# A norm's row factors fetched through DRAM, and the first unit's scaling moved behind its results

## The chip, the core and the metric

The kernel runs on one core of a Trainium2 chip. The time is device microseconds of one execution of the whole program, lower is better. Its matrix products are done by TensorE, elementwise work by VectorE, ScalarE and GpSimd; transfers are issued from the queues of SyncE (called SP), ScalarE and GpSimd (called POOL).

## What is computed

One layer of a hybrid encoder for 1024 rows of width 1024, all in float32. Three token mixers run on a normed input, are gated, summed and projected, and are added to the input; then comes a second norm and a convolutional gated mixer. The change lies where the second part begins:

```python
merged = (gates[:, :, 0] * (y_a @ w_br_hgrn) + gates[:, :, 1] * (y_b @ w_br_fox)
          + gates[:, :, 2] * (y_c @ w_br_mem))
x = x + merged @ w_out
h2 = x * rsqrt(mean(x * x, axis=-1) + EPS) * norm_ffn_g        # the second norm
a, v = split(h2 @ w_up, 2)                                     # the way up, 1024 -> 2 x 2816
a = causal_depthwise_conv3(a) + conv_b
x = x + (gelu(a) * v) @ w_down                                 # the way down
```

## The kernel before

Activations lie transposed: 128 channels on the partitions, the 1024 rows of the sequence along the free dimension, so a factor for each row of the sequence is a vector along the free dimension that every partition needs a copy of. That is `r2`, a tile of 128 x 1024 in which all partitions hold the same 1024 numbers. The norm is applied after the products: the way up multiplies the unnormed `x1` (times the norm's gain), and its results are multiplied by `r2`.

Each float32 operand is split into a rounded high part (a cast, mostly on ScalarE, line 166, or L166 through `operand_parts`) and a low part (a subtraction, mostly on VectorE, L174 or L1350), and one product is three matmuls (`mm3`, L160 to L162): high by high, and the two mixed ones. The weights' parts are the tiles `wh` and `wl`.

The way up goes in units. A unit makes two output blocks of 128 channels for all 1024 rows, by seven block products instead of eight (a scheme of Strassen's kind): the operands on the activations' side are seven families (`B11`, `T1`, `T2`, `B22`, `T3`, `B21`, `T4`), those on the weights' side `o1` to `o7`, sums of four blocks `a11`, `a12`, `a21`, `a22` that are loaded as the tile `rw`. One product is four blocks of `mm3`, 12 matmuls. There are 11 pairs of units; the first unit of a pair makes the convolution's rows (`at`, tiles `fa`), and the second the values (`put_v`). Results leave the PSUM banks through `put_a(c, n, ps, e)`, where `c` is the output block, `n` the half of the rows, `ps` the bank and `e` a copy of an earlier state of that bank. A bank goes on being added to after it was read: the product T4 adds to the bank that `put_a(1, 1, ...)` reads.

In the first unit things are drawn together. The products B11, T1 and T2 run while the last block of `x1` is still being finished; between T1 and T2, `second_norm` sums the squares (L1416, 8 products with a column of ones into 128 x 8) and `rstd_small` makes `rt2`, the factors as 8 columns of 128 (L178 on VectorE, L179 on GpSimd). `families` then makes the parts of the four other families. After the third, T3, `spread` makes `r2` from `rt2`: eight products of a column, broadcast along the free dimension, with the identity (L366), and two copies out of PSUM by ScalarE (L368). The rows `fa` lie where the first operands lay, so `new_rows` and all of `put_a` come after the families.

The order of instructions on each engine is written when the kernel is built, by a planner with a model of the times; program order is its priority. It is held in places by `tc.issue_after(ins)`, which keeps what follows behind `ins` on the engine of `ins`. In `families` T4 is kept behind the last operand of the first unit (`late["o7"]`), and the first operand of the second unit is kept behind the last low part of T4 (`late["last"]`). `acc`, the sum of squares, shares its tile with `r2`. The first norm's factors take a road through DRAM in `spread_dma` (L353 to L359): transposed to a row of 8 x 128, written, and read back to all partitions.

Of the kernel before, what the change touches and what calls it, by code (L numbers as in the profile page):

```python
# [8 lines left out]
F32 = mybir.dt.float32  # L9
F32R = mybir.dt.float32r  # L10
AF = mybir.ActivationFunctionType
ALU = mybir.AluOpType
AX = mybir.AxisListType

P = 128
T = 1024
D = 1024
KC = D // P
HB = 512
# [90 lines left out]
def tile_block(ctx: ExitStack, tc: tile.TileContext, xT, memT, x_rows, mem_rows, vec, fbias, mats, hmask, w_first, w_cm, w_hi, w_fqk, w_fv,  # L110
               w_mkv, w_br, w_out, w_up, w_dn, w_pair, outT):
    nc = tc.nc
    V, S, G, PE, SP = nc.vector, nc.scalar, nc.gpsimd, nc.tensor, nc.sync
# [17 lines left out]
    def ps_tr():  # L131
        return pz.tile([P, HB], F32, tag="tr", name="tr", bufs=2)

    def ps_po():
        return pz.tile([P, HB], F32, tag="po", name="po", bufs=1)
# [3 lines left out]
    ident = cp.tile([P, P], F32, tag="ident", name="ident")  # L139
# [36 lines left out]
    def rstd_small(out, ss, n):  # L176
        w = ss.shape[1]
        late["mean"] = V.tensor_scalar(out, ss, 1.0 / n, EPS, ALU.mult, ALU.add)  # L178
        return G.tensor_tensor(out, out, mhalf[:, :w], ALU.pow)  # L179
# [173 lines left out]
    def spread_dma(r, rcol, row, name, ps):  # L353
# [3 lines left out]
        rd = tc.dram_tile([1, T], F32, name=f"{name}_d")  # L357
        SP.dma_start(rd.rearrange("o (a b) -> (o a) b", a=8), row)
        SP.dma_start(r, rd.partition_broadcast(P))  # L359

    def spread(r, rcol):

        for n in range(2):
            ps = ps_tr()
            for b in range(4):
                PE.matmul(ps[:, b * P:(b + 1) * P], rcol[:, 4 * n + b:4 * n + b + 1].to_broadcast([P, P]), ident,  # L366
                          start=True, stop=True)
            S.copy(r[:, n * HB:(n + 1) * HB], ps)  # L368


    pkv = {}

# [131 lines left out]
    def family_block(name, k, src, sub=None):  # L504
        h, l = fam[name]
        return split(S, h[k], l[k], src, sub)
# [52 lines left out]
    class Dense:  # L559
# [11 lines left out]
        def sum_of(self, i, a, b, t=None):  # L571
            t = t if t is not None else home["sums"].tile([P, HB], F32, tag=f"s{i}", name=f"s{i}")
            V.tensor_add(t, a, b)
            return t

        def operand(self, src):
            if self.half is None:
                self.half = [wp.tile([P, 4 * 264], F32R, tag=t, name=t, bufs=3) for t in ("wh", "wl")]
                h, l = (t[:, :HB] for t in self.half)
            else:  # L580
                h, l = (t[:, HB:2 * HB] for t in self.half)
                self.half = None
            split(S, h, l, src)
            return h, l
# [746 lines left out]
    r2 = pr.tile([P, T], F32, tag="r2", name="r2")  # L1331
# [40 lines left out]
    for i, j in enumerate((0, 4, 1, 5, 2, 6, 3, 7)):  # L1372
# [6 lines left out]
        for n, ps in chunk:  # L1379
            sl = slice(n * HB, (n + 1) * HB)  # L1380
            dst = sum7 if i == 7 else x1[j]
# [29 lines left out]
    rt2 = cp.tile([P, 8], F32, tag="rt2", name="rt2")  # L1411

    def second_norm():
        ps = ps_po()
        for tb in range(8):
            PE.matmul(ps[:, tb:tb + 1], acc[:, tb * P:(tb + 1) * P], ones[:, 0:1], start=True, stop=True)  # L1416
        rstd_small(rt2, ps[:, :8], D)


    def snap(ps):  # L1420
# [4 lines left out]
    def first_products(o1, o2, o3, between=None):  # L1425
        x, y = ps_proj(), ps_lg()
        product(x, o1, "B11", True)
        e1 = snap(x)
        product(y, o2, "T1", True)
        e5 = snap(y)  # L1430
        late["e5"] = late["snap"]
        if between:
            between()
        product(x, o3, "T2", False)
        return x, y, e1, e5, snap(x)
# [16 lines left out]
    def unit(src, put, begun=None, before=None, after=None, ahead=None):  # L1452


        raw = pw.tile([P, 4, HB], F32, tag="rw", name="rw", bufs=2)
        for i in range(2):
            late["raw"] = G.dma_start(raw[:, 2 * i:2 * i + 2, :], src[:, 2 * i:2 * i + 2, :])  # L1457
        a11, a21, a22, a12 = (raw[:, i, :] for i in range(4))
        if begun:
            x, y, e1, e5, e2, o4 = begun  # L1460
            o5 = operand(sum_of(3, a11, a21))
            late["o5"] = late["cast"]
            o6, o7 = operand(a12), operand(a22)
            late["o7"] = late["cast"]
            before()
        else:
            with tc.issue_after(after.ins) if after else nullcontext():
                o1 = operand(a11)
                with tc.issue_after(late["split"].ins):
                    s1 = sum_of(1, a21, a22)  # L1470
                o2 = operand(s1)
            s2 = sum_of(2, s1, a11)
            x, y, e1, e5, e2 = first_products(o1, o2, operand(s2))
            o4 = operand(sum_of(4, s2, a12))
            o5 = operand(sum_of(3, a11, a21))
        product(y, o4, "B22", False)
        put(0, 1, y, e2)
        if not begun:
            o6 = operand(a12)
        product(x, o5, "T3", False)  # L1480
        put(1, 1, x, e5)
        if not begun:
            o7 = operand(a22)
        if ahead:
            ahead()
        z = ps_tr()
        product(z, o6, "B21", True)
        put(0, 0, z, e1)
        product(x, o7, "T4", False)
        put(1, 0, x, None)  # L1490
# [4 lines left out]
    def families():  # L1495

        for name, q, after in (("B22", 3, None), ("T3", 1, "e5"), ("B21", 2, "snap"), ("T4", 0, "snap")):
            with ExitStack() as order:
                if after:
                    order.enter_context(tc.issue_after(late[after].ins))  # L1500
                if after == "snap":
                    order.enter_context(tc.issue_after(late["split"].ins))
                    order.enter_context(tc.issue_after(late["o7" if name == "T4" else "o5"].ins))
                for k in range(4):
                    late["last"] = family_block(name, k, quarters(k)[q], G if name == "B21" and k > 1 else None)
            if name == "T3":
                spread(r2, rt2)
        px.release()
        late["pq"] = Rounded(tc, name="pq", bufs=1, side="right", reuse_waits="tile")

# [33 lines left out]
    for p in range(NF // 2):  # L1544
        at = []

        def new_rows():
            for _ in range(2):
                t = late["pq"].tile([P, T + 2], F32, tag="fa", name="fa", bufs=3)
                V.memset(t[:, 0:2], 0.0)  # L1550
                at.append(t)

        def rest():
            families()
            new_rows()

        def put_a(c, n, ps, e):
            sl = slice(n * HB, (n + 1) * HB)
            dst = at[c][:, 2 + n * HB:2 + (n + 1) * HB]
            src = ps  # L1560
            if e is not None:
                V.tensor_add(dst, ps, e)
                src = dst
            if c:
                V.scalar_tensor_tensor(out=dst, in0=src, scalar=-1.0, in1=r2[:, sl], op0=ALU.mult, op1=ALU.mult)
            else:
                V.tensor_mul(dst, src, r2[:, sl])

        if p:
            new_rows()  # L1570
            unit(w_up[2 * p], put_a)
            next(sums, None)
        else:
            unit(w_up[0], put_a, begun, rest)
        pq = late["pq"]
        cs = []
        for i in range(2):
            f = 2 * p + i
            c = pq.tile([P, T], F32, tag="fc", name="fc", bufs=4)
            w = [col(C_CW + t * NF + f) for t in range(3)]  # L1580
            S.activation(c, at[i][:, 2:], AF.Identity, bias=col(C_CB + f), scale=w[2])
            V.scalar_tensor_tensor(out=c, in0=at[i][:, 1:T + 1], scalar=w[1], in1=c, op0=ALU.mult, op1=ALU.add)
            V.scalar_tensor_tensor(out=c, in0=at[i][:, 0:T], scalar=w[0], in1=c, op0=ALU.mult, op1=ALU.add)
            S.activation(c, c, AF.Gelu)
            V.tensor_mul(c, c, r2)
            cs.append(c)

        def put_v(c, n, ps, e):
            dst = cs[c][:, n * HB:(n + 1) * HB]
            src = ps  # L1590
            if e is not None:
                V.tensor_add(e, ps, e)
                src = e
            if c:
                V.scalar_tensor_tensor(out=dst, in0=src, scalar=-1.0, in1=dst, op0=ALU.mult, op1=ALU.mult)
            else:
                V.tensor_mul(dst, src, dst)
            SP.dma_start(yd[:, 2 * c + n, p, :], dst)

        unit(w_up[2 * p + 1], put_v, after=None if p else late["last"],  # L1600
             ahead=down_operands if p == NF // 2 - 1 else None)
        for _ in range(1 + (1 <= p < 4)):
            next(sums, None)
        t1 = pq.tile([P, HB], F32, tag="ft", name="ft")
        V.tensor_sub(t1, cs[0][:, :HB], cs[0][:, HB:])
        SP.dma_start(yd[:, 4, p, :], t1)
# [62 lines left out]
    for a, b, own, first, c, n, sign, last, xq in (  # L1669
# [6 lines left out]
        dst = banks if own else ybanks  # L1676
# [138 lines left out]
```

## Time and profile before

| What | Value |
|---|---|
| Time, median of 3 runs | 1698.82 us (1698.47 to 1700.21) |
| The profiled execution's own time | 1700.23 us |
| Its span, first to last instruction | 1698.4 us |
| Granted TensorE clock over the span | 0.999 |
| TensorE busy | 1691.0 us |
| VectorE busy | 1150.8 us |
| ScalarE busy | 800.9 us |
| GpSimd busy | 324.6 us |

In the rows of the profile below, PE is TensorE, DVE is VectorE, ACT is ScalarE; "L366" is line 366 of the program. A row of a timeline gives start and length in us, engine, line, operation, output <- inputs and their shapes, and in brackets how long the engine idled before it and for whom. Tile names lose their numbers: `rt` stands for `rt2` too, `r` for `r2`, `x` for `x1`.

### The profile page before, as it was taken

The numbers are of one execution on the slowest core, as the hardware profiler recorded it, in microseconds if no ns is written. First come the engines' busy times: TensorE is split into PE (matmuls) and PEld (weight loads), VectorE is DVE, ScalarE is ACT, GpSimd is POOL, SyncE is SP. The second block draws the span as 40 slices with busy tenths as digits, with TensorE's granted clock in tenths as the row PEclk, the third lists the DMA queues.
The fourth block names the chain that finished last, engine by engine and source line by source line (L and its number), as shares of the span: only waits on it lengthen the run. The fifth ranks groups of instructions, "written<-read, shape, count | busy, mean of one in ns | idle before, by whom it ended". The sixth has DMA issues, their size and how long they took to land.

```text
span 1698.4 us, 24291 instructions
## 1 busy us (share of the span) xinstructions
PE 1691.0 (100%) x8957; PEld 1452.4 (86%) x8957; DVE 1150.8 (68%) x2057; ACT 800.9 (47%) x1428; POOL 324.6 (19%) x420
## 2 busy tenths in 40 slices
PE   9999999999999999999999999999999999999999
PEld 7888899989898998888888888888888888888887
DVE  6966455666666664886856845987878888775654
ACT  6734455545454553775631333644434444533432
POOL 0200032543433331544310000311111111100000
PEclk9999999999999999999999999999999999999999
DMA  9443232221212111110346542566544344494772
GB/s 367 157 161 106 88 139 68 77 92 51 94 59 77 63 46 57 67 32 13 106 127 209 167 186 100 165 174 169 158 139 138 118 149 143 172 363 145 251 269 87
DMA packets 83062, 227.16 MB, mean 134 GB/s; under 512 B 9712, under 2 KB 12408, under 8 KB 82816
## 3 DMA queue, kind: packets, MB, share of 16 engines
q1 hardware_dynamic: 64320, 160.54, 26.8%
q0 software_dynamic: 18048, 64.50, 13.2%
q8 instruction: 70, 1.15, 0.3%
q10 hardware_dynamic: 576, 0.59, 0.1%
q14 instruction: 48, 0.39, 0.1%
HBM read 180.72 MB, written 67.93 MB: 146 GB/s over the span
## 4 chain that ended last, share of the span: by engine, by line
PE 99%; DVE 0%; ACT 0%; DMA 0%; issue 0%; ACTq 0%; DVEq 0%
PE pp L160 21%; PE pp L162 21%; PE pp L161 21%; PE lg L160 4%; PE lg L162 4%; PE lg L161 4%; PE tr L162 3%; PE tr L161 3%; PE tr L160 3%; PE po L966 1%; PE lg L925 1%; PE lg L924 1%; PE po L965 1%; PE po L160 1%; PE po L161 1%; PE po L162 1%
## 5 line engine op out<-in xcount | busy, mean ns | idle before, releaser
L160 PE MATMUL pp<-uh,wh 128*128 128x512 f32 x412 | 163.3, 396 | 0.0
L161 PE MATMUL pp<-ul,wh 128*128 128x512 f32 x412 | 162.9, 395 | 0.0
L162 PE MATMUL pp<-uh,wl 128*128 128x512 f32 x412 | 162.5, 394 | 0.0
L161 PE MATMUL pp<-wl,uh 128*128 128x256 f32 (+1 forms) x512 | 146.3, 286 | 0.0
L162 PE MATMUL pp<-wh,ul 128*128 128x256 f32 (+1 forms) x512 | 146.1, 286 | 0.0
L160 PE MATMUL pp<-wh,uh 128*128 128x256 f32 (+1 forms) x512 | 145.6, 286 | 0.0
L166 ACT CAST wh<-s 128x512 fp32r<-128x512 f32 x110 | 66.5, 621 | 131.6 <-PE pp L161 55.1
L166 ACT CAST wh<-raw 128x1024 fp32r<-128x1024 f32 (+2 forms) x76 | 67.6, 890 | 100.6 <-PE pp L161 86.2
L166 ACT CAST wh<-rw 128x512 fp32r<-128x512 f32 x87 | 53.2, 619 | 108.1 <-PE pp L161 70.2
L160 PEld LDWEIGHTS pp<-wh,uh 128*128 128x128 f32 x512 | 97.3, 190 | 1.2
L161 PEld LDWEIGHTS pp<-wl,uh 128*128 128x128 f32 x512 | 97.4, 190 | 1.0
L162 PEld LDWEIGHTS pp<-wh,ul 128*128 128x128 f32 x512 | 97.4, 190 | 0.9
L1457 POOL DMA_DIRECT2D rw<-in_w_up x44 | 24.1, 555 | 372.4 <-DVE wl L1350 171.3
L166 ACT CAST dwh<-wr 128x1024 fp32r<-128x1024 f32 (+1 forms) x41 | 40.2, 980 | 115.8 <-PE tr L161 40.0
L162 PEld LDWEIGHTS pp<-uh,wl 128*128 128x128 f32 x412 | 77.5, 188 | 15.1
L174 DVE TENSOR_TENSOR wl<-raw,wh 128x1024 fp32r<-128x1024 f32 (+2 forms) x75 | 78.0, 1040 | 17.8 <-ACT wh L166 17.6
L160 PEld LDWEIGHTS pp<-uh,wh 128*128 128x128 f32 x412 | 77.5, 188 | 14.6
L161 PEld LDWEIGHTS pp<-ul,wh 128*128 128x128 f32 x412 | 77.5, 188 | 14.5
L940 ACT ACTIVATE pt<-pt,st 128x128 f32<-128x128 f32 (+3 forms) x64 | 49.7, 777 | 41.7 <-DVE st L937 33.9
L174 DVE TENSOR_TENSOR dwl<-wr,dwh 128x1024 fp32r<-128x1024 f32 (+1 forms) x41 | 46.3, 1129 | 31.7 <-ACT dwh L166 31.7
L942 POOL TENSOR_SCALAR pt<-pt,st 128x128 f32<-128x128 f32 (+3 forms) x64 | 49.1, 767 | 78.4 <-DVE st L941 64.1
L1350 DVE TENSOR_TENSOR wl<-rw,wh 128x512 fp32r<-128x512 f32 x69 | 47.7, 704 | 22.7 <-PE pp L162 18.2
(500 smaller groups left out, 5123.2 us busy)
## 6 DMA issues: line engine op xcount, KB each, us to landing
rw<-in_w_up POOLq DMA_DIRECT2D x44, 512.0 KB, 4.7
sd<-in_w_dn POOLq DMA_DIRECT2D x30, 512.0 KB, 6.0
br<-yd SPq DMA_DIRECT2D x30, 512.0 KB, 5.0
raw<-in_w_cm SPq DMA_DIRECT2D x24, 512.0 KB, 3.4
gd<-gt SPq DMA_DIRECT2D x48, 256.0 KB, 2.0
gt<-gd SPq DMA_DIRECT2D x48, 256.0 KB, 2.7
yd<-fc SPq DMA_DIRECT2D x44, 256.0 KB, 2.2
wr<-sd SPq DMA_DIRECT2D x20, 512.0 KB, 4.5
```

Source lines behind the costliest of these rows:

```text
L160: PE.matmul(ps, lh, rh, start=first, stop=False, skip_group_check=more)
L161: PE.matmul(ps, lh, rl, start=False, stop=False, skip_group_check=more)
L162: return PE.matmul(ps, ll, rh, start=False, stop=last, skip_group_check=more)
L166: return S.copy(out, in_)
L174: return (sub or V).tensor_sub(l, src, h.bitcast(F32))
L924: PE.matmul(ps[:, :w], qa[i][:, tsl], kh[i][:, s0:s0 + w], start=True, stop=False)
L925: fox_sets[p][3] = PE.matmul(ps[:, :w], qa[i][:, tsl], kl[i][:, s0:s0 + w], start=False, stop=True)
L940: S.activation(pt[:, :ns], pt[:, :ns], AF.Exp, bias=st[:, 2:3], accum_out=st[:, 3:4])
L942: G.tensor_scalar(pt[:, :ns], pt[:, :ns], st[:, 3:4], 0.0, ALU.mult, ALU.add)
L965: PE.matmul(o, vhl[:, sb, :], ph[:, src], start=(sb == 0), stop=False)
L1350: late["split"] = V.tensor_sub(l, src, h.bitcast(F32))
L1457: late["raw"] = G.dma_start(raw[:, 2 * i:2 * i + 2, :], src[:, 2 * i:2 * i + 2, :])
```

## The change

Three edits. `spread`, its eight products and its two copies go. `second_norm` instead writes `rt2` to a DRAM row of 1024 numbers, column by column, and reads that row back to all partitions as `r2`; both transfers are issued from SP. And in the first unit, `put_a` no longer multiplies by `r2`: it copies or adds into the row, and after the unit the two rows are multiplied whole, one of them with the sign turned. The other units are as before.

```diff
-    def spread(r, rcol):
-
-        for n in range(2):
-            ps = ps_tr()
-            for b in range(4):
-                PE.matmul(ps[:, b * P:(b + 1) * P], rcol[:, 4 * n + b:4 * n + b + 1].to_broadcast([P, P]), ident,
-                          start=True, stop=True)
-            S.copy(r[:, n * HB:(n + 1) * HB], ps)
...
         rstd_small(rt2, ps[:, :8], D)
+        rd = tc.dram_tile([1, T], F32, name="r2_d")
+        SP.dma_start(rd.rearrange("o (b p) -> (o p) b", p=P), rt2)
+        SP.dma_start(r2, rd.partition_broadcast(P))
...
-            if name == "T3":
-                spread(r2, rt2)
...
         def put_a(c, n, ps, e):
             sl = slice(n * HB, (n + 1) * HB)
             dst = at[c][:, 2 + n * HB:2 + (n + 1) * HB]
+            if p == 0:
+                if e is None:
+                    S.copy(dst, ps)
+                else:
+                    V.tensor_add(dst, ps, e)
+                return
...
             unit(w_up[0], put_a, begun, rest)
+            V.tensor_mul(at[0][:, 2:], at[0][:, 2:], r2)
+            V.scalar_tensor_tensor(out=at[1][:, 2:], in0=at[1][:, 2:], scalar=-1.0, in1=r2, op0=ALU.mult, op1=ALU.mult)
```

## The prediction

> **What bounds the kernel.** I read the page first: the busy rows and the chain of waits.
>
> ```profile
> span 1698.4 us, 24291 instructions
> ...
> PE 1691.0 (100%) x8957; PEld 1452.4 (86%) x8957; DVE 1150.8 (68%) x2057; ACT 800.9 (47%) x1428; POOL 324.6 (19%) x420
> ...
> PE 99%; DVE 0%; ACT 0%; DMA 0%; issue 0%; ACTq 0%; DVEq 0%
> ```
>
> TensorE is busy for all but 1698.4 - 1691.0 = 7.4 us, and the chain that ends last lies on it for 99% of the span. So whatever the change does to VectorE, ScalarE or the queues counts only if TensorE waits for it, and whatever it takes off TensorE counts in full, unless TensorE then waits for something else at that place. The second view is the list of stages.
>
> ```profile
> 1074.80:1089.00 14.20, 14.02 (x70) 11.45 (x69) 13.01 (x24) 7.68 (x16) 6.46 (x8) 1.00 0.68 194
> 1089.00:1113.00 24.00, 24.00 (x107) 19.88 (x106) 22.63 (x34) 13.75 (x21) 4.88 (x8) 1.00 0.76 198
> 1113.00:1200.00 87.00, 87.00 (x385) 72.06 (x384) 68.64 (x103) 35.46 (x54) 14.04 (x23) 1.00 0.61 168
> ```
>
> The columns are the stage's length, then the busy time of TensorE, weight load, VectorE, ScalarE and GpSimd, the granted clock, the DMA share and GB/s. The change works in the first two rows. There TensorE has one hole (14.20 - 14.02) and VectorE is nearly as full as TensorE: 13.01 of 14.20 us, then 22.63 of 24.00. So VectorE is the engine that could come to set the pace. Which wait ended last in that stage is told by the chain in order of time (start, length, owner), the third view.
>
> ```profile
> 1072.29 0.59 ACT fe L1422
> 1072.88 0.60 ACT wh L166
> 1073.47 2.09 ACT B21h L166 x4
> 1075.56 0.53 ACT wh L166
> 1076.15 0.51 issue
> 1076.89 1.77 DVE wl L1350
> 1079.19 0.68 DVE B21l L174
> 1079.87 2.41 DVE T4l L174 x4
> 1082.28 0.61 DVE wl L1350
> ```
>
> From 1072.29 to 1082.28 + 0.61 = 1082.89 the chain is not on TensorE at all. It leaves TensorE when the third product's result is out, goes through ScalarE's casts of the families and VectorE's low parts, and comes back with the low part `wl` of the second unit's first weights. The eight products of `spread` lie inside this stretch:
>
> ```profile
> 1077.30 0.39 PE L162 MATMUL pp<-T3h,wl 128*128 128x512 f32 x1
> 1077.53 1.95 PE L366 MATMUL tr<-ident,rt 128*128 128x128 f32 x16
> 1079.25 0.50 PE L160 MATMUL pp<-B11h,wh 128*128 128x512 f32 x1
> ...
> 1079.83 0.41 PE L160 MATMUL tr<-B21h,wh 128*128 128x512 f32 x1
> ...
> 1082.36 0.39 PE L162 MATMUL tr<-B21h,wl 128*128 128x512 f32 x1
> 1082.93 0.50 PE L162 MATMUL pp<-B11h,wl 128*128 128x512 f32 x1 [0.18 <-DVE wl L1350]
> ```
>
> Matmuls start 0.23 us apart (1077.30 to 1077.53), so the last row comes 1082.93 - 1082.36 - 0.23 = 0.34 us late, and its row names VectorE's `wl` as what it waited for.
>
> **Products taken out.** They hold TensorE from 1077.53 to 1079.25, which is 1.72 us, and the two matmuls behind them start a little slowly: 1077.53 to 1079.83 is 2.30 us, less 2 x 0.23 for these two, makes 1.84 us of TensorE time. Were it all on the path, the gain would be 1.84 us, and 2.18 with the 0.34 us.
>
> It is not on the path. What TensorE does next has its time set by VectorE:
>
> ```profile
> 1078.59 1.28 DVE L174 TENSOR_TENSOR B21l<-x,B21h 128x512 fp32r<-128x512 f32 x2
> ...
> 1082.20 0.68 DVE L1350 TENSOR_TENSOR wl<-rw,wh 128x512 fp32r<-128x512 f32 x1
> ```
>
> Without the spread the fourth product (B21) could start at about 1077.98 (1077.53 and the two fill-in matmuls). Its second matmul reads the low part of B21, whose first piece is done near 1079.2 (the chain's row of the second begins at 1079.19). Eleven matmuls from there end at 1079.3 + 11 x 0.23 = 1081.8. Then TensorE needs `wl`, which VectorE finishes at 1082.20 + 0.68 = 1082.88. Nothing ahead of this on VectorE or ScalarE reads r2 or waits for the spread, and the source pins that order: the family T4 is issued behind the seventh operand, and the first operand of the second unit behind `late["last"]`, the last low part of T4. Other work for TensorE isn't there: the product T4 adds to the bank that `put_a(1, 1)` has yet to read, and that read needs a tile in the place of rows that are free only when the last low part of T4 is made. So TensorE takes up `wl` at 1082.93 as before; the hole of 0.34 us grows by 1.84 us. Value taken for the removed products: 0 us; bounds 0 and -2.18.
>
> ScalarE's two copies of r2 out of PSUM (L368) also go. The next row of ScalarE behind them:
>
> ```profile
> 1083.51 0.62 ACT L166 CAST wh<-s 128x512 fp32r<-128x512 f32 x1 [3.35 <-DVE fa L1550]
> ```
>
> It stood idle for 3.35 us before this cast: 0 us.
>
> **Two transfers in their place.** On the SP queue nothing is near: the transfer that follows the new ones in it is issued at 1106.24.
>
> ```profile
> 1106.24 0.92 SPq L1598 DMA_DIRECT2D yd<-fc  x2
> ...
> 1071.70 2.65 POOL L179 TENSOR_TENSOR rt<-rt,mhalf 128x8 f32<-128x8 f32 x1 [2.63 <-DVE rt L178]
> ...
> 57.77 0.35 SPq L358 DMA_DIRECT2D rx_d<-line  x1
> 60.19 0.35 SPq L359 DMA_DIRECT2D rx<-rx_d  x1
> ...
> rx<-rx_d SPq DMA_DIRECT2D x1, 512.0 KB, 3.6
> ...
> fbr<-in_fbias SPq DMA_DIRECT2D x1, 4.0 KB, 5.0
> ...
> rw<-in_w_up POOLq DMA_DIRECT2D x44, 512.0 KB, 4.7
> ...
> t<-yd SPq DMA_DIRECT2D x1, 256.0 KB, 12.8
> ```
>
> The factors are ready at 1071.70 + 2.65 = 1074.35. The first norm goes the same road but from a row of 8 x 128: 2.42 us from the first issue to the second (57.77 to 60.19), then 3.6 to landing. By these rows r2 lands at 1074.35 + 2.42 + 3.6 = 1080.4, the early end. But here the write is 1024 separate words of 4 bytes, each 512 bytes apart from its partition's next, and nothing in this trace writes so. The nearest row in shape is `fbr`, also 128 x 8 words (5.0 us). The broadcast also runs beside loads of `rw` issued from 1078.96 on, so I give it their 4.7. Estimate: 1074.35 + 5.0 + 4.7 = 1084.1. As late end I take the longest landing in the list, 12.8, for the write: 1074.35 + 12.8 + 4.7 = 1091.9.
>
> **Scaling moved behind the unit.** The rows on VectorE now:
>
> ```profile
> 1085.23 0.68 DVE L1562 TENSOR_TENSOR fa<-tr,fe 128x512 f32<-128x512 f32 x1
> 1085.83 0.68 DVE L1567 TENSOR_TENSOR fa<-fa,r 128x512 f32<-128x512 f32 x1
> 1086.43 0.68 DVE L1350 TENSOR_TENSOR wl<-s,wh 128x512 fp32r<-128x512 f32 x1
> ...
> 1089.45 0.67 DVE L1565 SCALAR_TENSOR_TENSOR fa<-pp,r 128x512 f32<-128x512 f32 x1
> ...
> 1096.65 2.46 DVE L1583 SCALAR_TENSOR_TENSOR fc<-fa,cv,fc 128x1024 f32<-128x1024 f32 x2
> ...
> 1100.86 1.21 DVE L1585 TENSOR_TENSOR fc<-fc,r 128x1024 f32<-128x1024 f32 x1
> ...
> 1088.98 0.39 PE L162 MATMUL lg<-T1h,wl 128*128 128x512 f32 x1
> ```
>
> Four half rows scaled at 0.60 us each (1085.23, 1085.83, 1086.43: starts 0.60 apart) go, 2.4 us; a whole-row product like L1585 (1.21) and a whole-row scalar form like L1583 (2.46 / 2 = 1.23) come, 2.44 us. Net 0.0 on VectorE. ScalarE gains one copy of half a row (0.59 by the snap at 1072.29) and loses two: 0.
>
> The new product waits for r2 and for its row, which is complete at 1085.23 + 0.68 = 1085.9. With r2 at 1084.1 it does not wait. If it waits, everything behind it on VectorE waits, first the `wl` of 1086.43, done at 1087.1 now and read by TensorE at 1088.98: another 1.9 us of cover. So r2 may land as late as about 1087.1 before TensorE loses anything; my estimate leaves 3.0 us. Value: 0 us; bounds 0 and 1091.9 - 1087.1 = +4.8.
>
> Further on, TensorE is full in the rows of 1089 to 1200 and VectorE has a fifth of its time free from 1113 on, so nothing is gained or lost there by this sum.
>
> **Sum.** 0 + 0 + 0 = 0 us. The profiled execution took 1700.23 us, 1.83 beyond its span and 0.08% above the median, 1698.82, of three runs that lie 1.74 us (0.1%) apart. I forecast the median unchanged: 1698.8. As no change I count 0.2%, about what a measurement of this kernel can tell, that is 3.4 us.
>
> **Rivals.**
>
> 1. *The products' time is won.* If the planner, which writes the order anew, finds TensorE other work in the hole, or VectorE's `wl` comes sooner, 1.84 to 2.18 us go: about 1696.8. For it speaks that TensorE is otherwise 100% busy; against it the chain, which passes the products by, and the pinned order. Chance 0.13, all of it within 0.2%.
>
> 2. *The factors come late, and it is slower.* Place: the whole-row product at the head of VectorE's queue, with `wl` for T1 behind it. Price: one for one beyond the cover, landing minus 1087.1. With 4.7 for the broadcast it begins to cost when the write takes over 1087.1 - 4.7 - 1074.35 = 8.05 us and passes 0.2% at 11.4 us; at 12.8 it costs 4.8 us, 1703.6. For it: 1024 words where the first norm wrote 8 rows, a DMA share of 0.68 in this stage, and VectorE's queue full. Against it: the nearest rows take 2.4 and 5.0 us. Chance 0.22, of which 0.13 beyond 0.2%. The Trainium skill (DMA: Bandwidth & Descriptors, Rules for kernel authors) speaks against this write: a strided last dimension becomes one descriptor for each element, and one should make it contiguous. No run here shows yet what such a descriptor costs. The same page (Bandwidth, Measured) gives 0.68 us of transfer for 4 KB, which it calls a minimum of 64 packets at about 10.5 ns; by that, as an estimate, 64 words on each of 16 engines would cost under a microsecond more than the row form, r2 would land near 1081, and the sum would stay at zero.
>
> 3. *Another order later on.* The planner's changed times in this stage may shift the order of the ten later pairs of units. If each lost what this place loses now, 0.34 us and 0.12 for a slow restart as behind the spread (1.84 - 1.72), ten pairs give +4.6 us, 1703.4. Against it: TensorE is full from 1089 on while VectorE has room. A gain over 3.4 us needs nearly half of the 7.4 us in which TensorE idles anywhere in the span. Chance 0.17: 0.11 slower and 0.06 faster by over 0.2%.
>
> **How the numbers follow.** Forecast 0.48, rivals 0.13, 0.22, 0.17. Within 0.2%: 0.48 + 0.13 + 0.09 (the mild part of rival 2) = 0.70. Slower: 0.13 + 0.11 = 0.24. Faster: 0.06. The range reaches down to the whole gain of rival 1, 1698.8 - 2.2 = 1696.6, and up to 1703.4, near the late ends of rivals 2 and 3.
>
> **What would show it.** Right: no L366 rows; TensorE's wait for `wl` L1350 near 1082 grown from 0.2 to about 2 us; its last matmul of the span where it was; r2's broadcast landing between 1080 and 1087; VectorE's product without a wait for DMA. Rival 1: that TensorE wait not grown and the span 1.8 us shorter. Rival 2: VectorE waiting for DMA at r2, then TensorE for `wl`, behind 1087. Rival 3: new TensorE waits after 1113. The forecast is wrong if TensorE's holes outside 1077 to 1083 change by over a microsecond.

## The result

The changed kernel takes 1707.88 us (median of 6 runs, 1707.06 to 1709.12), the kernel before 1699.91 (6 runs, the three known ahead of the change among them): ratio 1.0049, 95% interval 1.0039 to 1.0060. It is slower by 8.0 us, where no change was forecast and 1703.4 was the top of the range. It went the way of the second rival, and further.

The stages of the changed kernel, with the columns as before (length, TensorE, weight load, VectorE, ScalarE, GpSimd, granted clock, DMA share, GB/s):

```profile
1074.80:1089.00 14.20, 12.46 (x54) 9.61 (x53) 10.59 (x19) 6.19 (x12) 5.68 (x7) 1.00 0.81 97
1089.00:1113.00 24.00, 18.59 (x77) 14.93 (x76) 18.41 (x25) 12.17 (x18) 4.37 (x7) 0.93 0.63 195
1113.00:1200.00 87.00, 87.00 (x386) 72.03 (x385) 71.32 (x108) 36.23 (x56) 14.52 (x24) 1.00 0.67 183
```

From 1113 on TensorE is full, as before. All that is lost is lost in the two stages that the change touches: TensorE is busy 5.4 us less between 1089 and 1113, the clock there is 0.93, and the DMA engines move 97 GB/s between 1074.8 and 1089 where they moved 194, though they are busier (0.81 for 0.68). The chain of waits, in order of time, says who set the pace:

```profile
1071.77 2.65 POOL rt L179
1074.44 13.02 DMA r_d<-rt
1087.54 6.78 DMA r<-r_d
1094.42 1.23 DVE fa L1572
1095.65 0.60 DVE s L1442
1096.25 0.61 DVE wl L1340
1096.91 0.79 PE pp L162
1097.70 0.43 PE pp L160
```

Where the chain of before ran over ScalarE's casts and the families, it now runs over the two new transfers: 13.02 us for 4 KB written word by word, then 6.78 for the broadcast. `r` lands at 1087.54 + 6.78 = 1094.3. TensorE's own rows with a wait in this stage, and the matmuls behind the last one:

```profile
1079.39 0.50 PE L161 MATMUL tr<-B21l,wh 128*128 128x512 f32 x1 [1.41 <-DVE B21l L174]
1083.00 0.50 PE L162 MATMUL pp<-B11h,wl 128*128 128x512 f32 x1 [0.33 <-DVE wl L1340]
...
1096.91 0.79 PE L162 MATMUL pp<-T2h,wl 128*128 128x512 f32 x1 [5.41 <-DVE wl L1340]
1097.50 0.63 PE L160 MATMUL pp<-T2h,wh 128*128 128x512 f32 x1
1097.92 0.63 PE L161 MATMUL pp<-T2l,wh 128*128 128x512 f32 x1
...
1100.64 0.39 PE L160 MATMUL tr<-B21h,wh 128*128 128x512 f32 x1
```

VectorE's two rows there, and below them the matmul of the kernel before that answers to the one at 1096.91:

```profile
1085.89 0.68 DVE L1340 TENSOR_TENSOR wl<-s,wh 128x512 fp32r<-128x512 f32 x1
1094.42 1.23 DVE L1572 TENSOR_TENSOR fa<-fa,r 128x1024 f32<-128x1024 f32 x1 [7.85 <-DMA r<-r_d]
```

```profile
1091.24 0.39 PE L162 MATMUL pp<-T2h,wl 128*128 128x512 f32 x1
```

VectorE stands idle for 7.85 us before the whole-row product, until `r` has landed.

Three things can be read in TensorE's rows. At 1079.39 and 1083.00 stand the holes into which the removed products went: TensorE takes up `wl` at 1083.00, before at 1082.93. The matmul T2 by `wl`, at 1091.24 in the kernel before, starts at 1096.91, 5.67 us later. And the ten matmuls from there to the next product take 1100.64 - 1096.91 = 3.73 us where ten cost 10 x 0.227 = 2.27: another 1.46 us, as the first of them start 0.43 us apart. Together 7.13 us; TensorE's last matmul of the span is 7.16 us later than before (1701.56 for 1694.40).

### The profile page after: what moved, and what is told of

It is laid out like the page before. It is cut to its first block, busy times and chain, and to the rows that moved or that the text cites. A ratio compares the mean times of both kernels' runs of the same rounds, so it can differ in the third digit from the quotient of the medians.

```text
span 1706.1 us, 24259 instructions
## 1 busy us (share of the span) xinstructions
PE 1691.2 (99%) x8941; PEld 1451.4 (85%) x8941; DVE 1150.6 (67%) x2055; ACT 800.0 (47%) x1427; POOL 327.0 (19%) x420
## 4 chain that ended last, share of the span: by engine, by line
PE 97%; DMA 1%; DVE 1%; POOL 0%; ACT 0%; issue 0%; ACTq 0%; SPq 0%; DVEq 0%
PE pp L160 21%; PE pp L162 21%; PE pp L161 21%; PE lg L160 4%; PE lg L161 4%; PE lg L162 4%; PE tr L161 3%; PE tr L162 3%; PE tr L160 3%; PE po L956 1%; PE lg L915 1%; PE lg L914 1%; PE po L955 1%; PE po L160 1%; PE po L161 1%; PE po L162 1%
## 5 line engine op out<-in xcount | busy, mean ns | idle before, releaser
L160 PEld LDWEIGHTS pp<-uh,wh 128*128 128x128 f32 x412 | 77.5, 188 | 14.6
```

What stands on the lines that cost most here:

```text
L160: PE.matmul(ps, lh, rh, start=first, stop=False, skip_group_check=more)
```

## The experiments

The theory was that the write by words alone makes the loss: r2 lands late, the whole-row product holds VectorE's queue, and the low part behind it holds TensorE. Rival A put the loss on the whole-row scaling or on the new order of instructions, rival C on the copies from DRAM to DRAM beside the write (the rows `sd`, sums of weights for the way down), rival D on the write's holding up the other transfers. The kernel before ran beside all of them (medians 1700.18 to 1700.42); each ratio is to it. A landing is read from the one profiled execution of each run.

| Run | Median us | Ratio, 95% interval | Write, issue to landing, us |
|---|---|---|---|
| e1, row of 8 x 512 bytes | 1701.42 | 1.0008 (0.9999 to 1.0017) | 2.1 (issue to next issue) |
| e2, whole rows alone | 1700.17 | 0.9999 (0.9990 to 1.0008) | none |
| e4, no write | 1700.76 | 1.0003 (0.9994 to 1.0012) | none |
| e6, 128 runs of 32 bytes | 1701.04 | 1.0006 (0.9997 to 1.0014) | 1.4 |
| e3, words written beside, unread | 1700.66 | 1.0001 (0.9993 to 1.0010) | 14.1 |
| e5, no copies near | 1707.07 | 1.0043 (1.0029 to 1.0057) | 9.6 |
| e9, words 64 bytes apart | 1700.64 | 1.0003 (0.9994 to 1.0013) | 5.2 |
| e13, half by words | 1712.66 | 1.0074 (1.0060 to 1.0088) | words at least 11.4; the runs behind them 14.6 |
| e14, sums in another order, runs of 32 bytes | 1702.59 | 1.0017 (1.0007 to 1.0026) | 1.4 |
| e15, e16, e17: words 32, 16, 8 bytes apart | one run each | | 5.3, 6.4, 8.9 |

**Is it the write, the scaling or the order?** Four runs.

e1 writes a row instead of words:

```diff
-        SP.dma_start(rd.rearrange("o (b p) -> (o p) b", p=P), rt2)
+        pst = ps_tr()
+        PE.transpose(pst[:8, :P], rt2, ident)
+        row2 = temp()[:8, :P]
+        S.copy(row2, pst[:8, :P])
+        SP.dma_start(rd.rearrange("o (a b) -> (o a) b", a=8), row2)
```

> The change with one thing different: the factors are first turned into a row of 8 x 128 (one transpose on TensorE, one small copy on ScalarE) and written as 8 pieces of 512 bytes instead of 1024 words. Theory (the write by words is the loss, 13.0 us from issue to landing): write about 2.4 us as at the first norm, r2 there before about 1087, VectorE's wait for r2 under 1 us, time within 1.5 us of the kernel before. Rival A (the whole-row scaling or the new order of instructions is the loss): TensorE's wait of 5.4 us stays in some form and the time stays near 1707.

e2 leaves the products and adds only the third edit:

> The kernel before, products of the spread kept, with only the third edit: the first unit's rows are scaled whole, after the unit. Theory: the same as before within 1 us, since VectorE does as much work as before. Rival A: the scaling itself is dear, 3 us or more slower.

e4 reads the broadcast from elsewhere:

```diff
-        SP.dma_start(rd.rearrange("o (b p) -> (o p) b", p=P), rt2)
-        SP.dma_start(r2, rd.partition_broadcast(P))
+        SP.dma_start(r2, w_dn[0:1, 0, 0:2, :].rearrange("o a b -> o (a b)").partition_broadcast(P))
```

> The change without the write by words: the broadcast reads a row of the down weights in DRAM (so the scaling has wrong numbers) and waits for nothing but its place. Theory: r2 lands before 1085, the 5.4 us wait and the slow matmuls behind it go, time within 1.5 us of the kernel before; and no gain from the products taken out, TensorE waits about 1.7 us more between 1077 and 1083 than before. Rival A: near 1707. Rival B (the products' time is worth something once r2 is early): 1.8 to 2.2 us faster than before.

e6 changes one line and no engine's order:

```diff
-        SP.dma_start(rd.rearrange("o (b p) -> (o p) b", p=P), rt2)
+        SP.dma_start(rd.rearrange("o (p b) -> (o p) b", p=P), rt2)
```

> The change, every engine's order of instructions unaltered; only the DRAM row is laid out so that each partition writes its 8 factors as one run of 32 bytes: 128 pieces instead of 1024 (r2 is then permuted, so the scaling has wrong numbers). Theory (the count of pieces sets the write's time): landing in under 5 us, r2 by about 1086, time within 1.5 us of the kernel before. Rival C (the write is slow because it runs beside the copies from DRAM to DRAM, whatever its pieces): landing still over 8 us and 4 us or more slower than before.

All four stand with the kernel before, none with 1707. So rival A falls: the scaling (e2) and the changed kernel's order without the products (e4) cost nothing that can be told from no change. e6 is the sharpest of them, since it has the changed kernel's instructions on every engine in the same order; only the layout of 4 KB in DRAM differs, and the loss is gone. The queue of SP, first of e6, then of the changed kernel:

```profile
1073.04 0.32 SPq L1409 DMA_DIRECT2D r_d<-rt  x1
1074.51 0.32 SPq L1410 DMA_DIRECT2D r<-r_d  x1
```

```profile
1074.44 0.38 SPq L1409 DMA_DIRECT2D r_d<-rt  x1
1087.54 0.33 SPq L1410 DMA_DIRECT2D r<-r_d  x1
```

The second issue waits for the first to land: 1.47 us in e6, 13.1 in the changed kernel. Where r2 is early, no time is won either; rival B of e4 (1.8 to 2.2 us faster) falls. e4's rows show where the removed products' time stayed:

```profile
1077.24 0.39 PE L162 MATMUL pp<-T3h,wl 128*128 128x512 f32 x1
1077.47 0.39 PE L160 MATMUL tr<-B21h,wh 128*128 128x512 f32 x1
1079.27 0.50 PE L161 MATMUL tr<-B21l,wh 128*128 128x512 f32 x1 [1.41 <-DVE B21l L174]
...
1082.88 0.50 PE L162 MATMUL pp<-B11h,wl 128*128 128x512 f32 x1 [0.33 <-DVE wl L1340]
```

Holes of 1.41 and 0.33 us stand in the place of 1.84 us of products, and `wl` is taken up at 1082.88, before at 1082.93. In e1 r2 lands too late for VectorE by 2.6 us (the broadcast took 8.8 beside the weight loads), which was expected to be under 1; TensorE's waits behind it stay within 0.4 us. The planner had put that product behind the low parts for T1 and T2 there.

**What makes the write slow?** Four runs.

e3 is the kernel before, with the same write and nobody to read it:

> The kernel before with one thing added: after the factors are made, the same 1024 words are written to DRAM, and nobody reads them; r2 still comes from the products. Theory (the write costs only because VectorE waits for what depends on it): the copies and weight loads beside it land late as in the changed kernel (about 13 and 10.5 us instead of 4 to 6), but nothing waits for them long enough, and the time is within 1.5 us of the kernel before. Rival D (the write costs by holding up the other transfers): 3 us or more slower, with a TensorE wait behind late weights.

e5 starts the copies later (`for _ in range((p > 0) + (1 <= p < 5))` for `range(1 + (1 <= p < 4))`):

> The change, with the copies from DRAM to DRAM for the way down begun one pair of units later, so that no such copy is in flight when the words are written (up to about 1080). Theory C1 (1024 words of 4 bytes are slow by themselves): landing stays near 13 us, 7 us or so slower than before. Theory C2 (words and the DRAM-to-DRAM copy hold each other up): landing falls below 6 us, r2 is there before 1088, and the time is within 1.5 us of the kernel before.

e9 gives each word 64 bytes:

```diff
-        SP.dma_start(rd.rearrange("o (b p) -> (o p) b", p=P), rt2)
-        SP.dma_start(r2, rd.partition_broadcast(P))
+        SP.dma_start(rd.rearrange("o (b p w) -> (o p) b w", p=P, w=16)[:, :, 0], rt2)
+        SP.dma_start(r2, rd[:, :T].partition_broadcast(P))
```

> The change, still 1024 words, but each word goes to a place of its own, 64 bytes from the next (the broadcast reads the first 4 KB, so the scaling has wrong numbers; the row is filled once, 60 us and more earlier, from a weight). Theory E1 (words that share a 64-byte piece of DRAM hold each other up): landing falls clearly, below 8 us. Theory E2 (the count of words sets the time): landing stays within 2 us of 13.

e13 writes half of the factors by words:

```diff
-        SP.dma_start(rd.rearrange("o (b p) -> (o p) b", p=P), rt2)
+        SP.dma_start(rd[:, :HB].rearrange("o (b p) -> (o p) b", p=P), rt2[:, :4])
+        SP.dma_start(rd[:, HB:].rearrange("o (p b) -> (o p) b", p=P), rt2[:, 4:])
```

> The change, with 512 of the factors written as words and the other 512 as 128 runs of 16 bytes in a second transfer (their order is permuted, so the scaling has wrong numbers). If the time goes with the count of words, the write takes about half, 6 to 8 us, r2 lands near 1088 and the time is 0 to 2 us over the kernel before; if it is a fixed price of any write by words, it stays near 13 us and 7 us slower.

e3's transfers in the window from 1073 to 1090, with the landing at the end of the row:

```profile
sd<-in_w_dn POOLq DMA_DIRECT2D x3, 512.0 KB, 13.5
rw<-in_w_up POOLq DMA_DIRECT2D x2, 512.0 KB, 11.5
r_d<-rt SPq DMA_DIRECT2D x1, 4.0 KB, 14.1
```

The weight loads `rw` beside the write take 11.5 us, 4.5 in the same window of the kernel before, and the time stays the same: rival D falls here, the held-up transfers have that much cover. The price is paid through r2 alone. The same answer for the changed kernel (1074 to 1094) and for e5 (1074 to 1098):

```profile
sd<-in_w_dn POOLq DMA_DIRECT2D x4, 512.0 KB, 9.8
rw<-in_w_up POOLq DMA_DIRECT2D x2, 512.0 KB, 10.5
r<-r_d SPq DMA_DIRECT2D x1, 512.0 KB, 6.8
r_d<-rt SPq DMA_DIRECT2D x1, 4.0 KB, 13.0
```

```profile
rw<-in_w_up POOLq DMA_DIRECT2D x2, 512.0 KB, 11.0
...
r<-r_d SPq DMA_DIRECT2D x1, 512.0 KB, 9.4
r_d<-rt SPq DMA_DIRECT2D x1, 4.0 KB, 9.6
```

In e5 the write takes 9.6 us: neither 13 (C1) nor under 6 (C2). So some 3 of the 13.0 us go with the company of the copies, and over 9 remain with hardly any (one copy is issued at 1080.3, before the words have landed). It brings nothing, since the weight loads issued at 1079.2 are held up too and the broadcast then takes 9.4: r2 lands at 1093.7, 0.6 us sooner.

With so little beside it, e5 also shows where the write's time isn't. This is the busy share of the 16 DMA engines in tenths, in 40 slices of 0.425 us from 1073 to 1090:

```profile
DMA  1000007300000000000000152311119217899999
```

The write's own packets lie in the slices from 1075.55 to 1076.40. Then the engines show nothing at all up to 1082.35, though weight loads were issued at 1079.2, and the write counts as landed only at 1084.2. So by far the most of the 9.6 us is not in the packets as the engines record them.

e9 decides between E1 and E2: as many words, to as many addresses, but 64 bytes apart, land in 5.2 us, and the loss is gone. e13's queue of SP says that the 14.6 us of its row must be read with care:

```profile
1074.22 0.37 SPq L1409 DMA_DIRECT2D r_d<-rt  x1
1074.64 0.50 SPq L1410 DMA_DIRECT2D r_d<-rt  x1
1089.48 0.32 SPq L1411 DMA_DIRECT2D r<-r_d  x1
```

The landing of 14.6 us is that of the second transfer, the 128 runs, which stand in the queue behind the words. The packets of the 512 words are all on record between 1075 and 1076, and those of the runs begin only at 1085.2. A transfer has landed with the last of its sixteen marks; for the words the trace holds fifteen, the last at 1085.59, so they took at least 11.4 us, where half of 13.0 would be 6.5. Neither expectation was met: it is not half the time, and at 12 us over the kernel before e13 is worse than the whole, because the broadcast is issued 1.9 us later than in the changed kernel and takes 9.2 us. So the count of words alone does not set the time; it matters how closely they lie together. The count has a price too: 1024 words 64 bytes apart take 5.2 us, 128 runs of 32 bytes 1.4.

**How does it depend on the distance?** The last three vary it, with e9's order of instructions:

> As the run with the words 64 bytes apart (landing 5.2 us), with the words 32 bytes apart, two in each 64 bytes of DRAM; same order of instructions, wrong numbers in the scaling. If neighbours in a 64-byte piece hold each other up: 5 to 8 us. If it is pieces of 32 bytes or fewer: 5.2 as before.

> As before, words 16 bytes apart, four in each 64 bytes. If neighbours hold each other up in proportion to their number: 6 to 9 us; if it is only the count of words: 5.2.

> As before, words 8 bytes apart, eight in each 64 bytes. By proportion: 8 to 12 us, on the way to the 13.0 of words 4 bytes apart.

Landing by distance of the words: 64 bytes 5.2 us, 32 bytes 5.3, 16 bytes 6.4, 8 bytes 8.9, and 4 bytes, as in the change, 13.0. Below 32 bytes it climbs as more words share a stretch; between 32 and 64 there is no difference, so two to a 64-byte piece do not yet hold each other up. Each is one landing, and the same write by neighbouring words took 13.0 us in the changed kernel and 14.1 in e3, so the step from 5.3 to 6.4 is no larger than such a difference; those to 8.9 and 13.0 are. Words further apart also spread the row over more DRAM, 64 KB in place of 4, and no run tells the two apart. What in the memory or in the DMA engines holds the words up, no run shows.

**A version in the change's spirit.** e14 sums other columns, so that a partition's factors are neighbours in the sequence and can be written as runs:

```diff
-            PE.matmul(ps[:, tb:tb + 1], acc[:, tb * P:(tb + 1) * P], ones[:, 0:1], start=True, stop=True)
+            PE.matmul(ps[:, tb:tb + 1], acc.rearrange("c (p b) -> c b p", b=8)[:, tb, :], ones[:, 0:1], start=True, stop=True)
...
-        SP.dma_start(rd.rearrange("o (b p) -> (o p) b", p=P), rt2)
+        SP.dma_start(rd.rearrange("o (p b) -> (o p) b", p=P), rt2)
```

> The change mended: the eight sums of squares take every eighth column instead of 128 neighbours, so that a partition's eight factors belong to eight neighbouring rows of the sequence, and each partition writes one run of 32 bytes to a row that is in the right order. Theory: write 1.4 to 3 us, r2 there before 1085, no wait of VectorE for it, time within 1.5 us of the kernel before; no faster, since TensorE then waits 1.4 and 0.3 us for B21's and the weights' low parts where the products were. Rival B: 1.8 us or more faster than before.

The write takes 1.4 us and nobody waits for r2, yet the kernel is 1.7 parts in a thousand slower than before (interval 0.7 to 2.6). The sums of squares have become dearer. Their weight loads, first of e14, then of the kernel before (operation, count, shortest, median, longest ns):

```profile
L1406 PEld LDWEIGHTS po<-ones,r x16: 316/335/336, 1068.0 to 1071.5; 128*128 128x128 f32 x16
```

```profile
L1416 PEld LDWEIGHTS po<-ones,r x16: 187/192/193, 1067.3 to 1070.5; 128*128 128x128 f32 x16
```

And their place among TensorE's rows, in the same order:

```profile
1068.18 3.74 PE L1406 MATMUL po<-ones,r 128*128 128x1 f32 x16
1071.78 0.47 PE L161 MATMUL pp<-T2l,wh 128*128 128x512 f32 x1
```

```profile
1067.54 0.95 PE L1416 MATMUL po<-ones,r 128*128 128x1 f32 x8
1068.35 0.49 PE L160 MATMUL pp<-T2h,wh 128*128 128x512 f32 x1
...
1069.83 0.95 PE L1416 MATMUL po<-ones,r 128*128 128x1 f32 x8
1070.64 0.48 PE L160 MATMUL pp<-T2h,wh 128*128 128x512 f32 x1
```

A weight load with a step of 32 bytes between its columns takes 335 ns where neighbours take 192. The sums hold TensorE for 1071.78 - 1068.18 = 3.60 us, before for 2 x 0.81 = 1.62, which is 1.98 us more, and the chain of both kernels passes through them. That fits most of the 2.4 us between the medians (1702.59 and 1700.18); it was not tried apart. No version that was run beats the kernel before.

## Why the prediction was wrong

**Right: the removed products are worth nothing.** Value 0 was taken, and e4 (1082.88) and the changed kernel (1083.00) take up `wl` within 0.1 us of its old place, 1082.93, with holes of 1.41 and 0.33 us. TensorE's wait at `wl` did not grow to 2 us as written; most of the wait came at B21's low part, whose place the text had worked out (1079.3) but not named as the wait. The two fill-in matmuls, which it put ahead of B21, came behind it.

**Right: the scaling.** VectorE's work came out even; e2, 0.9999.

**Wrong, the step that failed: the size of the write, in "Two transfers in their place".** I took 5.0 us from the landing of a load of 128 x 8 words and 12.8 as the late end, the longest landing in the list. The load's row was the nearest in shape, but each of its partitions moves one run of 32 bytes; what it resembles is e6, which took 1.4. The write by neighbouring words took 13.0, beyond the end that was thought safe. No row of the kernel before had the property that mattered, many short writes close together in DRAM. e9 is the test of this: its write takes 5.2 us, near what was taken, VectorE waits 0.2 us for r2, and the time is that of the kernel before, as forecast.

**Wrong, its neighbour: the broadcast.** 4.7 us taken, 6.8 measured. The 4.7 were those of a weight load by itself. Issued ahead of the two weight loads of that stage, the broadcast took 4.5 us (e4), 5.1 (e6) and 3.3 (e14); issued behind them, 8.8 (e1), 6.8 (e9 and the change), 9.4 (e5) and 9.2 (e13). In e1 and e9 those loads were hardly held up (4.4 and 5.6 us), so it isn't only the slow write that makes it dear. The late end was then not late enough in both terms: 1091.9 written, 1094.3 measured.

**Missing: the clock after a hole.** The loss was priced one for one. TensorE's hole of 5.41 us was followed by matmuls 0.43 us apart. The granted clock in the changed kernel from 1096.90 to 1099.60, and in e17, whose hole was 2.23 us, from 1092.00 to 1096.00 (the clock stands third from the end):

```profile
1096.90:1099.60 2.70, 2.69 (x6) 2.15 (x7) 2.58 (x4) 2.70 (x7) 0.00 (x0) 0.50 0.15 29
```

```profile
1092.00:1096.00 4.00, 2.03 (x9) 1.68 (x10) 3.83 (x6) 3.19 (x6) 0.00 (x0) 1.00 0.61 119
```

Half clock behind 5.41 us of idleness, full clock behind 2.23; in e5, behind 4.5 us, it was 0.56. The Trainium skill (TensorE: Matmul & The Clock Gate, Part 1) says that the array falls to half its clock after an idle window of about 3.4 us; the trace agrees, with 0.50 and 1.00 on either side of it. The slow matmuls make 1.46 of the 7.16 us.

**Where the cover ended.** It was set at 1087.1, by the low part for T1 behind the product. The planner put that low part ahead of the product (1085.89) and the one for T2 behind it (1096.16), which TensorE needs later, at 1091.2. That gave more cover: from 1094.42 the product (1.23), a sum (0.60) and the low part (0.61) end at 1096.9, so r2 could have landed about 5.6 us sooner, near 1088.7, without a loss. The mechanism of rival 2, which had been given 0.13 beyond 0.2%, was right in place and kind. Its price, landing minus 1087.1, would even have given 1094.3 - 1087.1 = 7.2 us, close to the 7.16 measured. That is luck: the cover reached 1.6 us further than written, and the slow matmuls, which were not in the price, made up for it.

On the page's rule that was weighed there: the Trainium skill (DMA: Bandwidth & Descriptors, Rules for kernel authors) advises against an element-wise last dimension, and the trace agrees with it: 13.0 us for words, 1.4 for runs of 32 bytes. The estimate from its figure for 4 KB, which is one of loads, was under a microsecond more than the row form and did not hold for this write: even words 64 bytes apart took 5.2 us.

## What to carry to other kernels

An operation that sits on the busiest engine can still be worth nothing: look for the stretch in which the chain leaves that engine, and work out what it would wait for once the operation is gone. A transfer whose like is not in the trace has no price there; ask in which property it differs from the rows at hand (here many short writes close together) and widen the range for that, or write runs instead of words. And when a wait on the busiest engine gets long, add the slow restart to its price.

## What was not expected of the hardware

1024 words written 4 bytes apart take 13.0 us, 64 bytes apart 5.2, and 512 of them 4 bytes apart still at least 11.4. In e5 the words' packets are done 7.8 us before the write has landed, and for 6 of these the DMA engines show nothing. While such a write is under way, loads of 512 KB beside it take 10.5 to 12.2 us for 4.5. A weight load with its columns 32 bytes apart takes 335 ns, with neighbouring columns 192.
